# Second-half router transposes in a fourth PSUM bank, a surplus branch amid the last up products, and two SBUF buffers claimed later, in a two-layer transformer with 16 experts

## Chip, cores, metric

One core of one Trainium2 chip. The metric is the device time of one execution in microseconds, the median of several runs: 846.9 us before (three runs, 843.6 to 847.3).

## What is computed

x is 256 tokens of width 1024, in float32. Two layers, each a mixer and a mixture of experts, each followed by a layer norm:

```
h = x @ w_in                       # projections for three kinds of attention, and gates
m = sum_i sigmoid(gate_i) * (attention_i @ w_branch_i)
x = LN1(alpha*x + m @ w_o)
aff  = sigmoid(x @ router_w)       # 16 experts in 4 groups: the best group, then its 2 best experts
y    = sum_e combine[:, e] * ((silu(x @ w_gate[e]) * (x @ w_up[e])) @ w_down[e])
x = LN2(alpha*x + y)
```

Each expert has 6 MB of weights, and all 16 are read in each layer.

## The kernel before

**Buffers.** SBUF holds 25 equal buffers of 1 MB (`slot`, line 229). They serve everything large: raw weights as loaded (kind "w") and intermediate tensors (kind "o"). The program counts both kinds. `pump` (line 299) issues weight loads in a fixed order as long as fewer than 25 minus `target["o"]` weight buffers are held, and `put` (line 308) gives buffers back and pumps. The counts decide where in the program a load stands. Which buffer it gets is decided by order of release: the one that was let go earliest in the program. All weight loads stand in SP's queue, in order; each waits there until the last reader of its buffer has finished.

**End of a mixer** (lines 845 to 896). The last product is `m @ w_o`, in the stages 58 and 59 of 60 at the end. Their products for tokens 0 to 127 (t=0) go first; VectorE adds the result to x (`added`) and takes statistics, GpSimd makes the reciprocal deviation, and meanwhile TensorE does the products for t=1. The router's logits (`logits`, line 783) are computed from x before the norm: TensorE transposes x in blocks of 128 columns into a PSUM bank (step 0), ScalarE copies them to SBUF (`xT`), and TensorE multiplies by the router weights (step 1). For the last half of t=1 the transposes go in two halves, since each half of x is ready at its own time. Both halves use one bank, pT[1]. There are four "mm" banks (`pmm`), two "sc" (`psc`) and two "tp" (`ptp`). `normed` (line 429) writes the normed x to zk with one ScalarE activation and copies it to x1h, rounded to float32r. The difference zk - x1h is x1l (`low`).

**Start of the experts** (`moe`, lines 961 to 1063). VectorE forms the affinities from the logits (aff), finds the chosen experts (msk), and from them the one-hot matrix Sx[0]; a product with the constant prev (pc) counts positions. ScalarE does the exponential and then the three other `normed` quarters. `gather` (line 1037) multiplies x1h and x1l by Sx to fetch each expert's tokens, up to 32 per 128 tokens. Results go to two buffers xe, evacuated in turn by ScalarE (even k) and VectorE (odd k). `warm` are transposes that fill TensorE's wait.

**Experts** (lines 1314 to 1374). The 16 experts go in pairs p = 0 to 7: gate products (`up_("g", p)`), up products (`up_("u", p)`), and the down products of the pair before (`down(p - 1)`). Each takes four buffers of 1 MB, in two steps q of two. `scatter` adds results back to the tokens; scatter(2, 0) and scatter(2, 1) are those of the pairs 4 and 5, both made during pair 7. At p = 7 `target["o"]` is set to 16, so few loads of the next layer stand before the layer's end.

**Surplus branch** (`over`, lines 1195 to 1247). If an expert has more than 32 tokens in a half, a branch on all engines recomputes the surplus. It isn't taken with these inputs. Each engine loads the flag, compares and jumps, and waits for its own earlier instructions; SP waits for all loads that it has issued. The branch claims a buffer (wov) and eight PSUM banks. In layer 0 it stands after pair 7's up products and scatter(2, 1), in layer 1 ahead of pair 7's gate products.

Of the kernel before, what the change touches and what calls it, by code (L numbers as in the profile page):

```python
# [20 lines left out]
T = 2  # L21
# [183 lines left out]
def kernel(ctx: ExitStack, tc: tile.TileContext, x, w_in, a_w_uk, a_w_uv, c_sinks, w_branch,  # L205
# [78 lines left out]
    def load_one(pieces=1):  # L284
        key, src, shape = loads[nxt[0]]
        nxt[0] += 1
        t = loaded[key] = slot(shape, F32, "w_" + "_".join(map(str, key)), kind="w")
# [141 lines left out]
    def normed(zk, x1h, sc, shs, t, k):  # L429

        xv, zv = xt[0].rearrange("p t (q k) -> p t q k", k=KD), zk.rearrange("p t k q -> p t q k")
        A.activation(zv[:, t, :, k:k + 4], xv[:, t, :, k:k + 4], AF.Identity, bias=shs[t], scale=sc[t][1])
        A.copy(x1h[:, t, k:k + 4], zk[:, t, k:k + 4])


    def mixer(l, todo):
# [346 lines left out]
        def logits(t, j, step, ks=range(4)):  # L783

            if step == 0:
                if ks[0] == 0:
                    pT[t], xT[t] = ptp(), work()
# [13 lines left out]
        for i, (c, q) in enumerate(stages):  # L801
# [43 lines left out]
            if i >= len(stages) - 2:  # L845

# [34 lines left out]
                x1h = slot([128, T, KD, 128], F32R, "x1h")  # L881
                normed(zk, x1h, sc, shs, 0, 0)
                for h in range(2):
                    for kk in range(2):
                        part(*tail[1], 1, kk, h)
                    added(1, slice(256 * h, 256 * h + 256), pa[c][1 + h][:, :256])
                halves = (range(2), range(2, 4))
                logits(1, 1, 0, halves[0])
                logits(0, 1, 1)
                logits(1, 1, 0, halves[1])  # L890
                logits(1, 1, 1, halves[0])
                logits(1, 1, 1, halves[1])
                sc += ln_scales(st[1:])
                shs.append(ln_shift(*sc[1], E=G, name="sh1"))
                drop(3)
# [65 lines left out]
    def moe(l, sc, shs, lg, rsum, zk, xh):  # L961
        target["o"] = 5
# [10 lines left out]
        z = [aff[:, NE * t:NE * t + NE] for t in range(T)]  # L973
        low(0, 0)
        for t in range(T):
            V.scalar_tensor_tensor(z[t], rsum[:, 0:NE], sc[t][0], lg[t][:, 0:NE], op0=OP.mult, op1=OP.subtract)
        for t in range(T):
            V.scalar_tensor_tensor(z[t], z[t], sc[t][1], rsum[:, NE:2 * NE], op0=OP.mult, op1=OP.subtract)
        A.activation(aff, aff, AF.Exp)
        for t, k in ((1, 0), (0, 4), (1, 4)):  # L980
            normed(zk, xh, sc, shs, t, k)
# [55 lines left out]
        def gather(r, ks=range(KD)):  # L1037

            if r not in xe:
                z = [slot([128, 4, 8, T, CAP], F32, "xe") for i in range(2)]  # L1040
                xe[r] = [z[k // 4][:, k % 4] for k in range(KD)]
            for k in ks:
                o = (ptp if k % 2 == 0 else psc)()
# [14 lines left out]
        target["o"] = 4  # L1058
        pump()
# [121 lines left out]
        def up_(nm, p, o):  # L1181
# [4 lines left out]
            for q in range(2):  # L1186
# [5 lines left out]
                if (nm, p, q) == ("g", 0, 0):  # L1192
                    gather(0, range(4, KD))

        def over():

            flag = nc.values_load(fi[0:1, 0:1], min_val=0, max_val=1)
            clk.on = False
            with tc.If(flag > 0, label=f"over{l}"):  # L1199
                cov = small(32, "cov")  # L1200
                ec, ce, o1, o2 = small(1, "ec"), small(2, "ce"), small(16, "o1"), small(16, "o2")
                wt4 = slot([128, 4, 512], F32, "wov")
                ws, xs = ([wt4[:, z + i] for i in range(2)] for z in (0, 2))
                pg, pu = [pmm(), pmm()], [pmm(), pmm()]
                pt, po = [ptp(), ptp()], [psc(), psc()]
                V.scalar_tensor_tensor(cov, pos, NEG * (1024 + cap), comb, op0=OP.is_lt, op1=OP.mult)
                V.memset(ec, 0.0)
                with tc.For_i(0, NE, 1) as e:
# [28 lines left out]
                    for n in range(2):  # L1237
# [7 lines left out]
                        for t in range(T):  # L1245
                            s = xt[0][:, t, 512 * n:512 * n + 512]
                            V.scalar_tensor_tensor(s, po[t], ce[:, t:t + 1], s, op0=OP.mult, op1=OP.add)

# [65 lines left out]
        for p in range(NE // 2):  # L1314
# [9 lines left out]
            if p == 7:  # L1324
                target["o"] = 16
                if l == depth - 1:
                    over()
                    drop(3)
                    clk.on = True
# [11 lines left out]
            if p == 7:  # L1341
                scatter(2, 0)
# [10 lines left out]
            if p == 7:  # L1353
                if l < depth - 1:
                    over()
                    drop(3)
                    clk.on = True
# [55 lines left out]
```

## Time and profile before

| what | value |
|---|---|
| median of three runs | 846.9 us (847.3, 846.9, 843.6) |
| the profiled execution | 840.26 us, span 838.3 us |
| granted TensorE clock, mean | 0.997 |
| TensorE busy | 810.7 us (97% of the span) |
| VectorE, ScalarE, GpSimd busy | 429.7, 293.2, 87.5 us |
| read from HBM | 263.39 MB, 315 GB/s over the span |

Times in the profile count from the span's start. In the names of tiles, w_g, w_u and w_d are gate, up and down weights, w_in the projections' weights, pm, ps and pt the PSUM banks of the three kinds, xt and acc the residual x in layers 0 and 1, wt the working tiles (xT among them), and cst the constants (a product pt<-cst alone is a warm transpose). PE is TensorE, DVE is VectorE, ACT is ScalarE, SP is the engine that issues the loads. A busy TensorE is not one at its peak.

### The profile page before, as it was taken

Reading aid. Unit: us, or ns where it says so; the run is one execution under the profiler, and the core shown is the slowest. Engines: PE = TensorE matmul, PEld = TensorE weight load, DVE = VectorE, ACT = ScalarE, POOL = GpSimd, SP = SyncE. Lnnn points to the kernel's source line nnn. Section 1 sums busy time; section 2 is a strip of 40 time slices with the busy share of each in tenths; the row PEclk is TensorE's granted clock in tenths of the full one; section 3 lists DMA queues with packets and bytes.
Section 4 is the critical chain, followed back from the end, with each engine's and each line's share of the span. In section 5 each row is a group of like instructions: output and inputs, shape, how many; then the busy total and the mean of one; then the engine's idle time right before and its main releaser. Section 6 shows DMA issues by size and latency. Waiting matters only on the chain.

```text
span 838.3 us, 11334 instructions
## 1 busy us (share of the span) xinstructions
PE 810.7 (97%) x4365; PEld 500.9 (60%) x4365; DVE 429.7 (51%) x896; ACT 293.2 (35%) x509; POOL 87.5 (10%) x88
## 2 busy tenths in 40 slices
PE   7999999999999999998999999999999999999986
PEld 7888778888443433332588877888874334333333
DVE  5898565785331323223489976549662422222244
ACT  5545667344211211100454476653341112111112
POOL 1222221000030000000122132100000200000001
PEclk9999999999999999999999999999999999999998
DMA  9993336994899999999899414478939999999992
GB/s 313 345 386 132 132 121 208 394 353 150 305 420 420 419 420 418 419 421 419 324 387 327 156 56 146 155 273 340 367 131 376 419 420 420 419 419 420 417 412 80
DMA packets 65115, 265.24 MB, mean 316 GB/s; under 512 B 6880, under 2 KB 11168, under 8 KB 40992
## 3 DMA queue, kind: packets, MB, share of 16 engines
q1 hardware_dynamic: 64912, 264.39, 80.8%
q8 instruction: 36, 0.59, 0.3%
q14 instruction: 23, 0.19, 0.1%
q10 hardware_dynamic: 144, 0.07, 0.0%
HBM read 263.39 MB, written 1.05 MB: 315 GB/s over the span
## 4 chain that ended last, share of the span: by engine, by line
PE 42%; DMA 7%; DVE 2%; ACT 1%; POOL 0%; issue 0%; POOLq 0%; SPq 0%; ACTq 0%
PE pm L163 35%; DMA w_d<-in_moe_w_down_dram 5%; PE pt L163 4%; PE ps L163 3%; DMA w_u<-in_moe_w_up_dram 2%; DVE bm L163 1%; DVE acc L163 1%; DVE hl L163 0%; POOLq L1409 0%; POOL acc L163 0%; ACT zk L163 0%; POOL rstd L163 0%; ACT hl L163 0%; ACT acc L163 0%; DVE mv L163 0%
## 5 line engine op out<-in xcount | busy, mean ns | idle before, releaser
L163 PE MATMUL pm<-hl,xh 128*128 128x512 f32 (+2 forms) x704 | 226.6, 389 | 1.5 <-ACT hl L163 1.3
L163 PEld LDWEIGHTS pm<-hl,xh 128*128 128x128 f32 x704 | 131.5, 189 | 29.1 <-issue 4.2
L163 DVE TENSOR_TENSOR hl<-w_in,hl 128x1024 fp32r<-128x1024 f32 (+2 forms) x86 | 104.8, 1228 | 60.3 <-ACT hl L163 57.7
L163 PE MATMUL pm<-hl,xl 128*128 128x512 f32 (+2 forms) x352 | 133.9, 380 | 0.3 <-DVE xl L163 0.3
L163 PE MATMUL pm<-w_d,he 128*64 128x512 f32 x512 | 119.4, 597 | 4.2 <-DVEq L1199 2.8
L163 PE MATMUL pm<-w_g,xe 128*64 128x512 f32 x512 | 115.3, 594 | 3.2 <-DVEq L1199 1.7
L163 PE MATMUL pm<-w_u,xe 128*64 128x512 f32 x512 | 114.9, 593 | 1.7 <-DMA w_u<-in_moe_w_up_dram 1.7
L163 ACT CAST hl<-w_in 128x1024 fp32r<-128x1024 f32 (+2 forms) x88 | 85.8, 1001 | 6.5 <-DMA w_in<-in_w_in_dram 5.7
L163 PEld LDWEIGHTS pm<-w_g,xe 128*64 128x64 f32 x512 | 36.9, 137 | 76.5 <-issue 71.2
L163 PEld LDWEIGHTS pm<-w_u,xe 128*64 128x64 f32 x512 | 37.8, 137 | 74.4 <-issue 69.0
L163 PEld LDWEIGHTS pm<-w_d,he 128*64 128x64 f32 x512 | 36.9, 137 | 72.9 <-issue 66.6
L163 PEld LDWEIGHTS pm<-hl,xl 128*128 128x128 f32 x352 | 66.9, 190 | 10.1 <-DVE xl L163 0.5
L163 DVE SCALAR_TENSOR_TENSOR he<-he,pm 128x512 f32<-128x512 f32 x16 | 17.0, 1063 | 87.6 <-ACT he L163 78.9
L163 DVE TENSOR_TENSOR he<-he,pm 128x512 f32<-128x512 f32 x16 | 17.1, 1069 | 67.4 <-PE pm L163 67.4
L163 ACT COPY he<-pm 128x512 f32<-128x512 f32 x14 | 8.2, 586 | 109.9 <-PE pm L163 109.9
L163 ACT ACTIVATE he<-pm 128x512 f32<-128x512 f32 x16 | 17.3, 1078 | 80.6 <-PE pm L163 80.6
L163 PE MATMUL pm<-hl,mh 128*128 128x512 f32 (+1 forms) x160 | 45.0, 355 | 0.0
L163 DVE SCALAR_TENSOR_TENSOR yt<-pm,cs,yt 128x512 fp32r<-128x512 f32 x32 | 22.9, 747 | 43.0 <-ACT yt L163 42.1
L163 ACT ACTIVATE yt<-pm,cs 128x512 fp32r<-128x512 f32 x32 | 20.8, 685 | 67.4 <-PE pm L163 67.4
L163 PE MATMUL pm<-hl,oh 128*128 128x512 f32 x128 | 41.3, 394 | 0.0
L163 POOL TENSOR_TENSOR un<-un,su 128x512 f32<-128x512 f32 x24 | 30.7, 1283 | 95.2 <-DVE su L163 57.0
L163 POOL TENSOR_TENSOR wt<-wt 128x256 f32<-128x256 f32 (+1 forms) x36 | 27.3, 772 | 107.5 <-DVE wt L163 99.9
(193 smaller groups left out, 989.9 us busy)
## 6 DMA issues: line engine op xcount, KB each, us to landing
w_g<-in_moe_w_gate_dram SPq DMA_DIRECT2D x64, 1024.0 KB, 13.7
w_u<-in_moe_w_up_dram SPq DMA_DIRECT2D x64, 1024.0 KB, 14.5
w_d<-in_moe_w_down_dram SPq DMA_DIRECT2D x60, 1024.0 KB, 19.1
w_in<-in_w_in_dram SPq DMA_DIRECT2D x36, 1024.0 KB, 13.5
w_br<-in_w_branch_dram SPq DMA_DIRECT2D x8, 1024.0 KB, 5.1
w_wo<-in_w_o_dram SPq DMA_DIRECT2D x8, 1024.0 KB, 5.1
w_d<-in_moe_w_down_dram SPq DMA_DIRECT2D x8, 512.0 KB, 17.1
w_in<-in_w_in_dram SPq DMA_DIRECT2D x4, 768.0 KB, 8.1
```

Of the source, the lines that this page charges most:

```text
L163: r = f(*args, **kw)
```

## The change

- In `logits`, the second half of t=1's transposes goes to a bank of its own, taken from the "mm" kind, and the products follow once for all four blocks.
- `normed` makes zk alone, with the two orders of its access pattern exchanged: it now writes zk contiguously and reads x with a stride of 8 elements, where before it read runs of 4 elements and wrote with a stride of 128. `high` makes x1h. For the first quarter, `high` stands behind the copies of the logits' transposes.
- x1h is claimed after the three buffers of the mixer's end are given back, and the first half and second half of xe are claimed one by one. `target["o"]` becomes 5 at the stages 58 and 59, and 4 at the start of `moe`, where it was 6 until the end of the mixer, 5 at the start of `moe` and 4 behind the first gather.
- In `moe` the four affinity operations of VectorE stand t by t ahead of low(0, 0), not behind it.
- scatter(2, 0) stands between the two steps of pair 7's gate products, and the branch between the two steps of its up products, in both layers. The branch's scratch counts as a weight buffer; the next layer's next load goes into it. Its accumulators share one bank more.

```diff
-    def load_one(pieces=1):
+    def load_one(pieces=1, t=None):
         key, src, shape = loads[nxt[0]]
         nxt[0] += 1
-        t = loaded[key] = slot(shape, F32, "w_" + "_".join(map(str, key)), kind="w")
+        if t is None:
+            t = slot(shape, F32, "w_" + "_".join(map(str, key)), kind="w")
+        else:
+            t = t.rearrange("p a b -> p (a b)")[:, :shape[1] * shape[2]].rearrange("p (a b) -> p a b", a=shape[1])
+        loaded[key] = t
...
-    def normed(zk, x1h, sc, shs, t, k):
-
-        xv, zv = xt[0].rearrange("p t (q k) -> p t q k", k=KD), zk.rearrange("p t k q -> p t q k")
-        A.activation(zv[:, t, :, k:k + 4], xv[:, t, :, k:k + 4], AF.Identity, bias=shs[t], scale=sc[t][1])
+    def normed(zk, sc, shs, t, k):
+
+        A.activation(zk[:, t, k:k + 4], xt[0][:, t].rearrange("p (q k) -> p k q", k=KD)[:, k:k + 4], AF.Identity,
+                     bias=shs[t], scale=sc[t][1])
+
+    def high(zk, x1h, t, k):
+
         A.copy(x1h[:, t, k:k + 4], zk[:, t, k:k + 4])
...
-        def logits(t, j, step, ks=range(4)):
+        def logits(t, j, step, ks=range(4), make=None):
 
             if step == 0:
                 if ks[0] == 0:
-                    pT[t], xT[t] = ptp(), work()
+                    xT[t] = work()
+                if ks[0] == 0 or make:
+                    pT[t] = (make or ptp)()
...
             if i >= len(stages) - 2:
+                target["o"] = 5
+                pump()
...
-                x1h = slot([128, T, KD, 128], F32R, "x1h")
-                normed(zk, x1h, sc, shs, 0, 0)
+                normed(zk, sc, shs, 0, 0)
                 for h in range(2):
                     for kk in range(2):
                         part(*tail[1], 1, kk, h)
                     added(1, slice(256 * h, 256 * h + 256), pa[c][1 + h][:, :256])
+                drop(3)
+                x1h = slot([128, T, KD, 128], F32R, "x1h")
                 halves = (range(2), range(2, 4))
                 logits(1, 1, 0, halves[0])
                 logits(0, 1, 1)
-                logits(1, 1, 0, halves[1])
-                logits(1, 1, 1, halves[0])
-                logits(1, 1, 1, halves[1])
+                logits(1, 1, 0, halves[1], pmm)
+                high(zk, x1h, 0, 0)
+                logits(1, 1, 1)
                 sc += ln_scales(st[1:])
                 shs.append(ln_shift(*sc[1], E=G, name="sh1"))
-                drop(3)
...
     def moe(l, sc, shs, lg, rsum, zk, xh):
-        target["o"] = 5
+        target["o"] = 4
...
-        low(0, 0)
-        for t in range(T):
-            V.scalar_tensor_tensor(z[t], rsum[:, 0:NE], sc[t][0], lg[t][:, 0:NE], op0=OP.mult, op1=OP.subtract)
-        for t in range(T):
-            V.scalar_tensor_tensor(z[t], z[t], sc[t][1], rsum[:, NE:2 * NE], op0=OP.mult, op1=OP.subtract)
-        A.activation(aff, aff, AF.Exp)
+        centred(0)
+        scaled(0)
+        centred(1)
+        scaled(1)
+        A.activation(aff, aff, AF.Exp)
+        low(0, 0)
...
-            if r not in xe:
-                z = [slot([128, 4, 8, T, CAP], F32, "xe") for i in range(2)]
-                xe[r] = [z[k // 4][:, k % 4] for k in range(KD)]
             for k in ks:
+                if k % 4 == 0:
+                    z = slot([128, 4, 8, T, CAP], F32, "xe")
+                    xe.setdefault(r, []).extend(z[:, i] for i in range(4))
...
-        target["o"] = 4
-        pump()
...
                 if (nm, p, q) == ("g", 0, 0):
                     gather(0, range(4, KD))
+                if (nm, p, q) == ("g", 7, 0):
+                    scatter(2, 0)
+                if (nm, p, q) == ("u", 7, 0):
+                    wt4 = over()
+                    drop(2)
+                    if l + 1 < depth:
+                        load_one(1, wt4)
+                    else:
+                        drop(1, "w")
+                    clk.on = True
 
         def over():
+            wt4 = slot([128, 4, 512], F32, "wov", kind="w")
...
-                wt4 = slot([128, 4, 512], F32, "wov")
-                pg, pu = [pmm(), pmm()], [pmm(), pmm()]
                 pt, po = [ptp(), ptp()], [psc(), psc()]
+                pg, pu = [pmm(), pmm()], [pmm(), po[1]]
...
             if p == 7:
                 target["o"] = 16
-                if l == depth - 1:
-                    over()
-                    drop(3)
-                    clk.on = True
...
-            if p == 7:
-                scatter(2, 0)
             up_("u", p, pu)
...
-            if p == 7:
-                if l < depth - 1:
-                    over()
-                    drop(3)
-                    clk.on = True
```

## Rows read from the trace of the kernel before

**Rows 1.** Busy time by stage: each stretch in us, its length, then busy time (and instructions) of PE, PEld (weight loads), DVE, ACT and POOL, the granted clock, the DMA engines' share and GB/s. The stretches are the mixer's end and the experts' start, the experts with TensorE never idle, and the experts' end, for layer 0 and then (without the second) layer 1.
```profile
194.00:222.00 28.00, 26.93 (x189) 20.50 (x190) 14.31 (x48) 12.44 (x17) 1.70 (x4) 1.00 0.51 180
222.00:360.00 138.00, 138.00 (x716) 53.13 (x714) 39.32 (x61) 20.74 (x29) 7.52 (x2) 1.00 1.01 417
360.00:410.00 50.00, 44.84 (x226) 16.20 (x224) 15.60 (x21) 6.69 (x9) 0.00 (x0) 1.00 0.98 397
606.00:634.00 28.00, 26.94 (x188) 20.80 (x189) 14.32 (x48) 12.34 (x18) 1.68 (x4) 1.00 0.52 183
...
780.00:818.00 38.00, 34.20 (x171) 13.31 (x164) 14.76 (x20) 6.31 (x8) 0.00 (x0) 1.00 1.01 413
```

**Rows 2.** Who waited for whom, for TensorE over the whole span: us in total, times, longest. DVEq L1199 is VectorE's sequencer at the surplus branch.
```profile
PE pm L163 <- DVEq L1199: 4.5, 2, 2.8
...
PE pt L163 <- ACT wt L163: 1.9, 2, 1.0
```

**Rows 3.** TensorE in order of time, at the experts' start of layer 0: start and duration in us, and in brackets the idle time before and what ended it. The last line is the same place in layer 1.
```profile
201.26 0.96 PE L163 MATMUL ps<-rwg,wt 128*128 128x16 f32 x8
203.18 0.44 PE L163 MATMUL pt<-cst,xt 128*128 128x128 f32 x2 [0.96 <-ACT wt L163]
...
210.17 0.28 PE L163 MATMUL pt<-Sx,x1l 128*128 128x256 f32 x1
...
211.85 0.65 PE L163 MATMUL pm<-w_g,xe 128*64 128x512 f32 x2
...
615.85 0.44 PE L163 MATMUL pt<-cst,acc 128*128 128x128 f32 x2 [0.95 <-ACT wt L163]
```

**Rows 4.** ScalarE in order of time, same place in layer 0.
```profile
199.80 0.59 ACT L163 COPY wt<-pt 128x512 f32<-128x512 f32 x1 [5.88 <-PE pt L163]
200.93 1.28 ACT L163 ACTIVATE zk<-xt,sh,rstd 128x512 f32<-128x512 f32 x1 [0.54 <-DVE xt L163]
202.24 0.62 ACT L163 CAST x1h<-zk 128x512 fp32r<-128x512 f32 x1
202.76 0.36 ACT L163 COPY wt<-pt 128x256 f32<-128x256 f32 x1
203.66 0.37 ACT L163 COPY wt<-pt 128x256 f32<-128x256 f32 x1 [0.53 <-PE pt L163]
205.34 0.23 ACT L163 ACTIVATE aff<-aff 128x32 f32<-128x32 f32 x1 [1.31 <-DVE aff L163]
...
211.02 1.44 ACT L163 ACTIVATE xe<-pt,gpk 128x512 f32<-128x512 f32 x2
```

**Rows 5.** VectorE in order of time, same place in layer 0.
```profile
201.31 0.41 DVE L163 SCALAR_TENSOR_TENSOR xt<-xt,pm 128x256 f32<-128x256 f32 x1
...
202.89 0.69 DVE L163 TENSOR_TENSOR x1l<-zk,x1h 128x512 fp32r<-128x512 f32 x1 [0.23 <-ACT x1h L163]
...
204.74 0.23 DVE L163 SCALAR_TENSOR_TENSOR aff<-rsum,mv,ps 128x16 f32<-128x16 f32 x1 [1.01 <-PE ps L163]
204.89 0.42 DVE L163 SCALAR_TENSOR_TENSOR aff<-aff,rstd,rsum 128x16 f32<-128x16 f32 x2
205.61 0.18 DVE L163 TENSOR_SCALAR aff<-aff 128x32 f32<-128x32 f32 x1 [0.30 <-ACT aff L163]
```

**Rows 6.** SP in order of time: single loads (the last one of w_d for pair 0, and two of w_g for pair 2, layer 0), and the first load of layer 1's w_in behind the branch.
```profile
201.10 0.33 SPq L221 DMA_DIRECT2D w_d<-in_moe_w_down_dram  x1
...
210.49 0.33 SPq L221 DMA_DIRECT2D w_g<-in_moe_w_gate_dram  x1
...
221.22 0.33 SPq L221 DMA_DIRECT2D w_g<-in_moe_w_gate_dram  x1
...
409.96 0.38 SPq L221 DMA_DIRECT2D w_in<-in_w_in_dram  x1
```

**Rows 7.** TensorE's weight products in order of time, pair 7 and the down products of pairs 6 and 7, layer 0.
```profile
377.22 3.65 PE L163 MATMUL pm<-w_g,xe 128*64 128x512 f32 x14 [1.33 <-DMA w_g<-in_moe_w_gate_dram]
...
387.36 3.65 PE L163 MATMUL pm<-w_u,xe 128*64 128x512 f32 x14 [0.92 <-DMA w_u<-in_moe_w_up_dram]
394.91 0.65 PE L163 MATMUL pm<-w_d,he 128*64 128x512 f32 x2 [2.75 <-DVEq L1199]
...
408.15 1.08 PE L163 MATMUL pm<-w_d,he 128*64 128x512 f32 x4
```

**Rows 8.** The same for layer 1.
```profile
785.72 7.95 PE L163 MATMUL pm<-w_g,xe 128*64 128x512 f32 x32 [1.70 <-DVEq L1199]
...
800.00 3.65 PE L163 MATMUL pm<-w_u,xe 128*64 128x512 f32 x14 [0.76 <-DMA w_u<-in_moe_w_up_dram]
...
814.99 1.51 PE L163 MATMUL pm<-w_d,he 128*64 128x512 f32 x6 [1.34 <-DMA w_d<-in_moe_w_down_dram]
```

**Rows 9.** Groups of instructions over the whole span, shapes apart: busy us in total, mean ns of one, idle time before and what ended it. The first writes he with a stride, the second writes it contiguously; the third reads two scale operands and writes contiguously, and the last reads x1h and x1l with a stride, on GpSimd.
```profile
L163 ACT ACTIVATE he<-pm 128x512 f32<-128x512 f32 x16 | 17.3, 1078 | 80.6 <-PE pm L163 80.6
...
L163 ACT COPY he<-pm 128x512 f32<-128x512 f32 x14 | 8.2, 586 | 109.9 <-PE pm L163 109.9
...
L163 ACT ACTIVATE xe<-pt,gpk 128x512 f32<-128x512 f32 x16 | 12.2, 776 | 21.7 <-PE pt L163 21.7
...
L163 POOL TENSOR_TENSOR acc<-x1h,x1l 128x1024 f32<-128x1024 f32 x4 | 15.1, 3783 | 62.6 <-PE pm L163 62.6
```

More of the change, by code (lines that the diff above doesn't have):

```diff
@@ L973, in moe, with centred, scaled @@
         z = [aff[:, NE * t:NE * t + NE] for t in range(T)]
-        low(0, 0)
-        for t in range(T):
-            V.scalar_tensor_tensor(z[t], rsum[:, 0:NE], sc[t][0], lg[t][:, 0:NE], op0=OP.mult, op1=OP.subtract)
-        for t in range(T):
-            V.scalar_tensor_tensor(z[t], z[t], sc[t][1], rsum[:, NE:2 * NE], op0=OP.mult, op1=OP.subtract)
-        A.activation(aff, aff, AF.Exp)
+        def centred(t):
+            V.scalar_tensor_tensor(z[t], rsum[:, 0:NE], sc[t][0], lg[t][:, 0:NE], op0=OP.mult, op1=OP.subtract)
+        def scaled(t):
+            V.scalar_tensor_tensor(z[t], z[t], sc[t][1], rsum[:, NE:2 * NE], op0=OP.mult, op1=OP.subtract)
+        centred(0)
[3 more added lines that the diff above has]
+        A.activation(aff, aff, AF.Exp)
+        low(0, 0)
         for t, k in ((1, 0), (0, 4), (1, 4)):
-            normed(zk, xh, sc, shs, t, k)
+            normed(zk, sc, shs, t, k)
+            high(zk, xh, t, k)
         drop()
@@ L1247, in over @@
                             V.scalar_tensor_tensor(s, po[t], ce[:, t:t + 1], s, op0=OP.mult, op1=OP.add)
+            return wt4
         o, parts, stm = {}, [], []
```

## The prediction, made before the changed kernel was run

> **What bounds the kernel now.** I read the busy time by stage first. TensorE is busy for 97% of the span, so only stages where it idles can give anything. Those are the passages from mixer to experts (1.1 us idle of 28 in each layer) and the experts' ends (5.2 us of 50 in layer 0, 3.8 of 38 in layer 1) [rows 1]. In the experts' stretches the reader should look at the last two columns: the DMA engines are full and move 413 to 417 GB/s, so a 1 MB buffer (1.049 MB) lands every 2.5 us. In the passages they are half empty (180 GB/s).
>
> Next, TensorE's waits: 4.5 us for VectorE at the surplus branch, and 1.9 us for ScalarE's copies of the logits' transposes [rows 2].
>
> Then the engines in order of time. At the passage TensorE waits 0.96 us for the copy that frees the shared bank [rows 3]. From there one chain sets the experts' start: ScalarE's copy (203.66), the logits, VectorE's affinities (204.74), the exponential (205.34), then ScalarE without a pause through three normed quarters to the first xe (211.02), and the first gate product at 211.85 [rows 3 to 5].
>
> At the experts' ends TensorE has caught up with the loads: it resumes at 377.22, 387.36, 800.00 and 814.99 on a landing [rows 7, 8].
>
> So the experts are bound like this: the load at 221.22 waits for a buffer that TensorE's gate products of pair 0 let go [rows 6]. From the landing of this load on the DMA engines are full until the layer's end. The end is therefore the experts' start plus a fixed time, and **a microsecond off the start is a microsecond off the end**, while one saved at the end mostly runs into the next landing.
>
> **The change part by part.**
>
> *Logits' bank.* Before, ScalarE's order is zk (ends 202.21), x1h, the copy of the first half, a wait for TensorE, the copy of the second [rows 4]. Now the second half's transposes need only x, ready at 201.72 [rows 5], and TensorE, free at 203.18 - 0.96 = 202.22 [rows 3]; they end at 202.66. The first copy moves up to 202.24, the second goes at 202.70 instead of 203.66: 0.96 us gained. x1h (0.62 us) follows at 203.07, in ScalarE's wait for the affinities (1.31 us before [rows 4]).
>
> *Affinities.* They come at 203.78 instead of 204.74. One of the two scaled operations (the pair takes 0.42 us [rows 5]) now precedes the logits' arrival, so 0.15 to 0.2 us more leaves the chain. The exponential goes at about 204.2, 1.1 us earlier.
>
> *low(0, 0) behind them.* This adds a wait: it takes 0.69 us of VectorE [rows 5] ahead of the next affinity operation, which then starts at about 204.9 instead of 205.61, 0.7 earlier. Behind it stand the choice of experts, Sx and the gather: its first block, done at 210.45 [rows 3], would be done at 209.75. ScalarE reaches xe at 211.02 - 1.1 = 209.92, still last. So VectorE's smaller gain is covered, by 0.2 us. With 0.8 us of xe behind it, the gate products start at 210.75 instead of 211.85.
>
> *zk's access pattern.* ScalarE's contiguous write takes 586 ns, the same size with a strided write 1078, so the stride costs 0.49 us [rows 9]. zk takes 1.28 [rows 4]; the contiguous activation with two scale operands, 776 ns [rows 9], plus 0.49 is 1.27, so reading runs of four costs nothing. The trace has no ScalarE operation with a strided read. The nearest rows: 776 ns if it is free; on GpSimd two strided reads take 3783 ns for 1024 columns, 1.89 us for 512 [rows 9], the upper end. I take 1.28, unchanged, a single stride's price as for the write. At 776 ns the normed chain shrinks by 1.5 us, but VectorE's gather (209.75) then bounds: 0.2 us more per layer. At 1.89 us zk stands four times in the chain: 4 x 0.61 = 2.4 us, less the 0.1 of slack that the first copy leaves: 2.3 us per layer lost.
>
> The Trainium skill (SBUF — State Buffer, section "Door 1: The DMA port swizzle", the note on 16-byte cachelines) says that each access to a new line pays and four fp32 values share one. By that, the read with a stride of 32 bytes pays as the write did, and the sum stays as below; taken as free, it would be 0.4 us lower over both layers.
>
> *Buffers and loads.* The last w_d of pair 0 is issued earlier than 201.10, behind stage 57, and the first w_g of pair 2 at about 201.3 instead of 210.49 [rows 6], as their buffers are let go by the mixer's last products. The load after these waits for zk's last reader, and the one at 221.22 for pair 0's gate products, as before: the number of weight buffers from the first gather on is the same. So two loads move within an idle stretch of the DMA engines, and the saturated stream starts with the same load. Worth nothing by itself. New waits: zk takes stage 58's buffer, last read ahead of the transposes copied at 199.80 [rows 4]; x1h that of the mixer's low part, read until TensorE's logits; xe's first half that of x, read until ScalarE's last zk. All end before they are asked for. GpSimd's queue isn't passed.
>
> *scatter(2, 0)* goes into a stretch where TensorE idles 1.33 us for w_g [rows 7]; the next step resumes on a landing anyway. Nothing in either layer.
>
> *The branch.* It frees TensorE of 2.75 us at 394.91 and 1.70 at 785.72 [rows 7, 8]. In its new place VectorE reaches it right after pair 7's gate activation, ahead of TensorE's first use of a bank behind it. TensorE's own part, between 0 and 1.70 us (the whole idle time in layer 1 [rows 8]), I put at 0.5, low in that span since VectorE is named as the one that ended both waits; 0.92 and 0.76 us of waiting for w_u cover it [rows 7, 8]; uncovered it costs what exceeds them. What is late next: in layer 0 the loads. The last w_u lands at 387.3, the next four at 2.5 us each: 397.3 for w_d of pair 6, 402.3 for the second buffer of pair 7. The down products then go at 402.3 + 3.6 + 1.9 (the rest's products) = 407.8 instead of 408.15 [rows 7]: 0.3 us of 2.75. In layer 1 the wait for w_d at 814.99 takes all 1.70. SP's branch stands behind the same load as before, so it waits for the same landings, and the first load behind it, now into the scratch, keeps its place at 409.96 [rows 6].
>
> *Sum.* 1.1 us at each experts' start (the row at 615.85 shows the same wait in layer 1 [rows 3]) and 0.3 at layer 0's end: 2.5 us. The profiled execution's 840.3 us would be 837.8. It is 6.6 us below the median of the runs, so I take the difference: 846.9 - 2.5 = **844.4 us**. A measurement of this kernel tells 0.5%, 4.2 us, from no change; this is less.
>
> **The rivals.**
>
> *The early loads pay.* If moving them up by 8 to 9 us really advanced the stream by one buffer, each layer's end would come 2.5 us earlier, covered by the idle 5.2 and 3.8 us there [rows 1]: 2 x 2.5 more, 839.4. For it: half-empty DMA engines in the passage. Against it: the load at 221.22 waits for TensorE, not for the queue.
>
> *The strided read is dearer.* The place is zk, four times per layer in the chain. At 1.89 us: 2 x 2.3 - 2.5 = 2.1 us slower, 849.0. It decides from about 1.6 us on, where 2 x 4 x 0.3 = 2.4 us eat the gain. For it: GpSimd's row. Against it: one read here, two there, and another engine.
>
> *The branch in mid-product stalls TensorE.* The Trainium skill (Runtime: NRT & Kernel Launch, "Instruction fetch mechanics") says that a taken branch whose target isn't in the two pages held waits for a fetch. No row shows a stall of its own: what there is lies within the 1.70 us. As a mechanism here: 1.70 instead of 0.5 exceeds the cover by 0.8 and 0.9 us, which layer 0 gives back out of the freed 2.75 and layer 1 out of the 1.34 us ahead of 814.99 [rows 8]. Time: 844.4 to 844.7. It shows in the trace rather than in the time.
>
> *The change does less than it says:* if the second transposes still waited for the first copy, in spite of their own bank, only x1h's 0.52 us ahead of the copies and the 0.15 of the affinities would go per layer: 2 x 0.67 + 0.3 = 1.6, 845.3.
>
> **How the numbers follow.** My forecast has 0.62, the stall 0.06, the early loads 0.12, the dearer read 0.12, the lesser change 0.08. Runs of one kernel spread over 3.7 us, so a case's measured time lies within some 2 us of it. Low: 840.8 leaves out the lower part of the early loads' case. High: 848.5 leaves out the upper half of the dearer read's. Faster by over 0.5%: the early loads nearly whole (0.11) and 0.11 of the forecast by the spread, 0.22. Slower by over 0.5% (above 851.1): the dearer read at its upper end with the spread, 0.04. Within: 0.74.
>
> **What would show it.** Right: TensorE's 0.96 us wait before the second transposes gone; two ScalarE copies back to back ahead of x1h; the first gate product 1.1 us earlier against the mixer's last product in both layers; no DVEq wait at the branch, but longer waits for w_d instead. Wrong: zk not near 1.28 us; the stretch from the first gate product to the layer's end not the same to 0.4 us; a wait of over 1 us in mid up product of pair 7.

## The result and the profile after

| | median us | runs | lowest to highest |
|---|---|---|---|
| before | 846.86 | 6 | 840.6 to 847.3 |
| after | 839.44 | 6 | 838.56 to 840.89 |

The ratio of the runs is 0.9935, with an interval of 0.9905 to 0.9964: faster by 0.65%. By these two medians it is 7.4 us. The forecast was 844.4 us (840.8 to 848.5). The ratio puts the kernel after at 841.4 us against the 846.9 that the forecast started from, inside the range; the median of its own runs lies 1.4 us below it. The likeliest case, a change within 0.5%, is neither met nor ruled out: the interval reaches from 0.36 to 0.95% faster. One run of the kernel before, at 1178.99 us with a mean clock of 0.654, is left out of every figure below.

The two profiled executions say something else: their spans are 838.4 us (after) and 838.3 us (before). The question is why the profiles agree and the medians differ.

First the busy time by stage of the kernel after, in the columns and stretches of [rows 1].

```profile
194.00:222.00 28.00, 27.93 (x194) 21.15 (x194) 14.25 (x48) 13.13 (x18) 1.66 (x4) 1.00 0.50 185
222.00:360.00 138.00, 138.00 (x716) 53.14 (x712) 39.32 (x61) 20.72 (x29) 7.53 (x2) 1.00 1.01 417
360.00:410.00 50.00, 47.40 (x226) 18.06 (x224) 15.79 (x21) 6.94 (x10) 0.00 (x0) 1.00 0.98 397
606.00:634.00 28.00, 27.95 (x197) 21.72 (x197) 14.25 (x48) 12.95 (x18) 1.64 (x4) 1.00 0.53 186
780.00:818.00 38.00, 35.44 (x171) 13.35 (x168) 14.84 (x20) 6.27 (x8) 0.00 (x0) 1.00 1.01 413
```

TensorE's idle time at the passages is gone (1.07 to 0.07 us in layer 0), and at the experts' ends it falls from 5.2 to 2.6 us and from 3.8 to 2.6. Next, the passage in order of time: TensorE (the last two lines are layer 1), then ScalarE, then VectorE. These answer to [rows 3 to 5].

```profile
202.09 0.96 PE L163 MATMUL ps<-rwg,wt 128*128 128x16 f32 x8
202.90 0.42 PE L163 MATMUL pm<-cst,xt 128*128 128x128 f32 x2
...
210.13 0.28 PE L163 MATMUL pt<-Sx,x1l 128*128 128x256 f32 x1
...
211.80 1.08 PE L163 MATMUL pm<-w_g,xe 128*64 128x512 f32 x4
...
615.77 0.42 PE L163 MATMUL pm<-cst,acc 128*128 128x128 f32 x2
...
624.63 1.94 PE L163 MATMUL pm<-w_g,xe 128*64 128x512 f32 x8
```

```profile
201.76 1.32 ACT L163 ACTIVATE zk<-xt,sh,rstd 128x512 f32<-128x512 f32 x1 [0.55 <-DVE xt L163]
202.98 0.35 ACT L163 COPY wt<-pt 128x256 f32<-128x256 f32 x1
203.36 0.37 ACT L163 COPY wt<-pm 128x256 f32<-128x256 f32 x1
203.62 0.62 ACT L163 CAST x1h<-zk 128x512 fp32r<-128x512 f32 x1
205.09 0.23 ACT L163 ACTIVATE aff<-aff 128x32 f32<-128x32 f32 x1 [0.85 <-DVE aff L163]
...
210.91 1.44 ACT L163 ACTIVATE xe<-pt,gpk 128x512 f32<-128x512 f32 x2
```

```profile
204.83 0.23 DVE L163 SCALAR_TENSOR_TENSOR aff<-aff,rstd,rsum 128x16 f32<-128x16 f32 x1
204.98 0.68 DVE L163 TENSOR_TENSOR x1l<-zk,x1h 128x512 fp32r<-128x512 f32 x1
205.58 0.17 DVE L163 TENSOR_SCALAR aff<-aff 128x32 f32<-128x32 f32 x1
```

Times must be taken from a common point, because this execution arrives at the passage 0.83 us late (zk at 201.76, not 200.93 [rows 4]). From zk to the exponential are 3.33 us instead of 4.41, to xe 9.15 instead of 10.09, to the first gate product 10.04 instead of 10.92. So the exponential gains 1.08 us and the gate products 0.88. TensorE's second transposes no longer wait, and the two copies stand back to back ahead of x1h.

TensorE at the experts' ends (layer 0, then layer 1), against [rows 7, 8]:

```profile
386.14 4.70 PE L163 MATMUL pm<-w_u,xe 128*64 128x512 f32 x16 [0.28 <-PEq L1228]
...
402.21 3.65 PE L163 MATMUL pm<-w_d,he 128*64 128x512 f32 x14 [1.36 <-DMA w_d<-in_moe_w_down_dram]
...
407.83 3.65 PE L163 MATMUL pm<-w_d,he 128*64 128x512 f32 x16
...
795.05 8.62 PE L163 MATMUL pm<-w_u,xe 128*64 128x512 f32 x30 [0.77 <-DMA w_u<-in_moe_w_up_dram]
...
815.01 3.65 PE L163 MATMUL pm<-w_d,he 128*64 128x512 f32 x14 [1.33 <-DMA w_d<-in_moe_w_down_dram]
```

No wait names VectorE's sequencer any more. At the branch TensorE is idle for 0.28 us in layer 0. That isn't all of its price: the row at 795.05, with the branch in it, takes 8.62 us for 30 products, where [rows 8] has 32 in 7.95. A wait of 1.36 us for w_d has come in layer 0, and that of layer 1 is unchanged. From the first gate product to the last down step, layer 0 takes 196.03 us instead of 196.30.

Then the granted clock behind layer 1's start (windows of 4 us, columns as above), and TensorE there:

```profile
418.00:422.00 4.00, 2.49 (x20) 1.95 (x18) 3.96 (x6) 1.89 (x4) 2.88 (x2) 1.00 1.05 388
422.00:426.00 4.00, 3.69 (x15) 3.25 (x15) 2.17 (x4) 0.85 (x2) 0.00 (x0) 0.57 1.04 386
```

```profile
420.97 0.63 PE L163 MATMUL pt<-cst,acc 128*128 128x128 f32 x4 [1.51 <-DVE acc L163]
...
423.43 0.74 PE L163 MATMUL pm<-hl,xh 128*128 128x324 f32 x2
```

The granted clock is 0.57 on average over these 4 us: most of them at the lower level, 1.2 GHz. Pairs of products that take 0.46 us at the full clock take 0.74. TensorE had just been idle for 1.51 us. The profiled execution of before had the same idle stretch and kept its clock:

```profile
421.29 0.63 PE L163 MATMUL pt<-cst,acc 128*128 128x128 f32 x4 [1.51 <-DVE acc L163]
```

```profile
422.00:426.00 4.00, 3.46 (x24) 2.96 (x23) 2.62 (x5) 1.92 (x4) 0.28 (x1) 1.00 1.04 387
```

So the profiles balance like this (after minus before): 0.83 us lost in the first 15 us, where the programs are identical; 0.88 gained at layer 0's passage; 0.27 at its end; 1.35 lost from there to layer 1's passage; 0.91 gained at that passage (10.81 us before, 9.90 after, from the first of the logits' last transposes to the gate product); 0.10 at layer 1's end. The sum is 0.02 us lost, with over 2 us won by the change.

The 0.83 us at the start are the clock's too. TensorE's first transposes and products of each execution go at the lower level: a pair of products takes 0.74 us there, as in the fall above, and 0.46 a little later. The level rises at another moment in each execution. TensorE around that moment, before and then after:

```profile
9.98 0.74 PE L163 MATMUL pm<-hl,xh 128*128 128x324 f32 x2
...
11.06 1.07 PE L163 MATMUL pt<-cst,xt 128*128 128x128 f32 x8
...
12.27 0.45 PE L163 MATMUL pm<-hl,xh 128*128 128x324 f32 x2
```

```profile
11.11 1.80 PE L163 MATMUL pt<-cst,xt 128*128 128x128 f32 x8
```

The same eight transposes take 1.07 us in one execution and 1.80 in the other. The column of the clock shows 1.00 throughout, because the trace's record of the clock begins only with the rise, at 11.12 us before and 12.65 after. In all twelve profiles the record begins between 10.53 and 13.67 us, and the first zk starts between 200.64 and 202.22: about half a microsecond later for each microsecond that the rise comes later.

### The profile page after: what moved, and what is told of

The parts are those of the page before. It is cut to its first block, busy times and chain, and to the rows that moved or that the text cites. A ratio compares the mean times of both kernels' runs of the same rounds, so it can differ in the third digit from the quotient of the medians.

```text
span 838.4 us, 11339 instructions
## 1 busy us (share of the span) xinstructions
PE 816.8 (97%) x4365; PEld 504.7 (60%) x4365; DVE 430.0 (51%) x896; ACT 293.5 (35%) x509; POOL 87.6 (10%) x88
## 4 chain that ended last, share of the span: by engine, by line
PE 81%; DMA 15%; DVE 2%; ACT 1%; POOL 0%; issue 0%; POOLq 0%; SPq 0%; ACTq 0%
PE pm L163 68%; DMA w_d<-in_moe_w_down_dram 9%; PE pt L163 8%; PE ps L163 5%; DMA w_u<-in_moe_w_up_dram 5%; DVE bm L163 1%; DVE hl L163 1%; DVE acc L163 1%; DMA cst<-in_consts_dram 0%; ACT hl L163 0%; ACT zk L163 0%; POOLq L1427 0%; POOL acc L163 0%; POOL rstd L163 0%; DVE ml L163 0%
## 5 line engine op out<-in xcount | busy, mean ns | idle before, releaser
L163 DVE TENSOR_TENSOR hl<-w_in,hl 128x1024 fp32r<-128x1024 f32 (+2 forms) x84 | 103.1, 1238 | 60.4 <-ACT hl L163 57.7
L163 PE MATMUL pm<-w_u,xe 128*64 128x512 f32 x512 | 117.3, 593 | 2.1 <-DMA w_u<-in_moe_w_up_dram 1.5
## 6 DMA issues: line engine op xcount, KB each, us to landing
w_g<-in_moe_w_gate_dram SPq DMA_DIRECT2D x64, 1024.0 KB, 13.7
```

The costliest lines, as they stand in the source:

```text
L163: r = f(*args, **kw)
```

## The experiments

**First: which part, and do the runs differ by the clock?** Four kernels: before once more, and each of the three parts alone on top of before. *Passage* has the change's `normed`, `high` and `logits`, and `low(0, 0)` behind the affinities; in its core:

```diff
-                logits(1, 1, 0, halves[1])
-                logits(1, 1, 1, halves[0])
-                logits(1, 1, 1, halves[1])
+                logits(1, 1, 0, halves[1], pmm)
+                high(zk, x1h, 0, 0)
+                logits(1, 1, 1)
```

*Branch* has the change's `up_` and `over`:

```diff
+                if (nm, p, q) == ("g", 7, 0):
+                    scatter(2, 0)
+                if (nm, p, q) == ("u", 7, 0):
+                    wt4 = over()
```

*Loads* has the change's targets, and its claims of x1h and xe:

```diff
+                target["o"] = 5
+                pump()
...
-        target["o"] = 5
+        target["o"] = 4
```

> The kernel before once more, unchanged, for the granted clock and the time of each of its runs (the runs listed so far give 840.6 to 847.3 us and no clock). Three theories on why the change gains 7 us by the medians and only 2.5 us by my sum. Theory of the clock: in some executions the granted clock falls to its lower level for about 3.4 us behind an idle stretch of TensorE (the trace of after has one such fall, at 422 us, behind 1.51 us of idle, and the trace of before has none). One fall of 3.4 us at half speed takes 1.7 us off the work and 0.002 off the mean clock (1.7 of 838); then runs near 847 us should show a mean clock 0.006 to 0.008 lower than runs near 840 us, and the times should lie on steps of about 1.3 to 1.7 us. Theory of the stream: in the runs of 847 us weights land later, TensorE waits for them at the same clock: the mean clock differs by less than 0.002 between runs of 840 and of 847 us. Theory of the chain alone: the scatter is chance and the medians differ by 2 to 3 us once more runs are taken, here a median near 843 us.

> The kernel before with one part of the change alone: the logits in two PSUM banks, the copy of the states behind the logits' copies, low(0, 0) behind the affinities and the exchanged access patterns of zk; loads and branch stay where they were. Chain alone: 0.9 us less per layer, so 1.8 us below the kernel before, 845.1 at a median of 846.9. Clock: the 0.96 and 0.95 us waits ahead of the second transposes go, but the branch's 2.75 and 1.70 us stay, so it may lose some falls of the clock at the two passages: 1.8 us and up to two falls of 1.3 to 1.7, 842 to 845. Stream: 0 to 1.8 us, as without the loads' earlier start nothing lands earlier.

> The kernel before with the surplus branch and scatter(2, 0) moved amid the up products and the scratch in the next weights' buffer, nothing else. Chain alone: 0.3 us in layer 0 and 0 to 0.1 in layer 1, so 846.5 at a median of 846.9. Clock: TensorE's idle of 2.75 and 1.70 us goes, and with it the falls behind them: if most of the extra 5 us hangs on these two places, 842 to 844; a fall behind each costs 1.3 to 1.7 us, so two falls give no more than 3.4. Stream: 846.9, unchanged to 0.3.

> The kernel before with the claims and loads alone: targets 5 and 4, the pump at the two stages, x1h claimed behind the drop, the halves of xe claimed one by one; logits, copies and branch as before. Chain alone and clock: no gain, 846.9 to within 0.5 (two loads start 7 to 8 us earlier and land long before they are read). Stream: the two weights per layer that start 7 to 8 us earlier let the whole stream run ahead: 840 to 842.

| kernel | median us | lowest to highest | ratio to before (interval) | mean clock of the runs |
|---|---|---|---|---|
| before again | 843.64 | 840.24 to 847.54 | 0.9998 (0.9972 to 1.0024) | 0.988 to 0.997 |
| passage | 841.06 | 840.46 to 841.65 | 0.9957 (0.9935 to 0.9979) | 0.992 to 0.996 |
| branch | 842.29 | 840.28 to 845.01 | 0.9976 (0.9954 to 0.9998) | 0.992 to 0.998 |
| loads | 842.83 | 840.22 to 847.64 | 0.9981 (0.9954 to 1.0009) | 0.988 to 0.997 |

The runs of the kernel before lie on three steps, and the mean clock names the step. Over all 104 runs of it taken with these experiments, 23 lie at 840.05 to 841.55 us (mean clock 0.997 to 0.998), 48 at 842.66 to 844.89 (0.993 to 0.995), and 33 at 846.14 to 847.87 (0.988 to 0.991). The theory of the stream needed the same clock on all steps, so it falls. This time the profile fell on the middle step. Windows of the kernel before, run again (843.28 us), with the two idle stretches ahead of the falls:

```profile
204.00:208.00 4.00, 4.00 (x25) 4.00 (x25) 3.01 (x20) 2.91 (x4) 0.00 (x0) 0.64 0.22 90
208.00:212.00 4.00, 4.00 (x34) 3.84 (x33) 1.68 (x6) 2.86 (x5) 0.00 (x0) 0.94 0.26 47
...
396.00:400.00 4.00, 3.90 (x11) 1.47 (x13) 0.00 (x0) 0.00 (x0) 0.00 (x0) 0.57 1.03 416
```

```profile
202.90 0.44 PE L163 MATMUL pt<-cst,xt 128*128 128x128 f32 x2 [0.97 <-ACT wt L163]
...
213.20 1.08 PE L163 MATMUL pm<-w_g,xe 128*64 128x512 f32 x4
...
396.10 1.89 PE L163 MATMUL pm<-w_d,he 128*64 128x512 f32 x4 [2.76 <-DVEq L1199]
```

From the second transposes to the first gate product it takes 10.30 us instead of 8.67 [rows 3]: one fall costs 1.6 us there. The first profile of before has the same idle stretch [rows 3] and no fall behind it. Two falls make 843.3 out of 840.4. The top step would be four by its mean clock; none of the profiled executions lies on it.

The loads alone keep all three steps (five, four and three runs), and their lowest runs are those of before: **the early loads are worth nothing.** The branch alone keeps two steps of six runs each, 840.41 and 844.14 us in the middle; its profile has a fall behind the 0.97 us of layer 0's passage and one of double length behind layer 1's 0.96 us:

```profile
618.00:622.00 4.00, 3.89 (x19) 3.80 (x19) 2.26 (x13) 2.24 (x5) 0.00 (x0) 0.52 0.37 152
622.00:626.00 4.00, 4.00 (x25) 4.00 (x24) 1.59 (x10) 3.54 (x4) 0.00 (x0) 0.63 0.07 14
```

The passage alone has no run above 841.65, yet none below 840.46 either, and none at 0.997. Here the mean clock does not name the time: five runs at 0.992 to 0.994 and seven at 0.996 lie at 841.2 and 841.0 us in the middle. Its profile (841.65) has falls at the two places that it leaves: the branch, and layer 1's start (windows of 4 us):

```profile
392.00:396.00 4.00, 2.01 (x6) 0.86 (x8) 1.73 (x3) 0.00 (x0) 0.00 (x0) 0.69 1.02 416
...
422.00:426.00 4.00, 3.46 (x18) 2.92 (x17) 2.97 (x5) 1.22 (x2) 0.75 (x1) 0.78 1.05 388
```

**Second: the clock by itself, the bank, and a better version.** In *cover* nothing of the change is done; the idle stretches of before are only filled:

```diff
             turn_x(0, t)
+            if l > 0 and t == 0:
+                warm(12, pmm)
...
                 logits(0, 1, 1)
+                warm(8, pmm)
                 logits(1, 1, 0, halves[1])
...
                 if l == depth - 1:
+                    warm(12, pmm)
                     over()
...
                 if l < depth - 1:
+                    warm(20, pmm)
                     over()
```

*No bank* is after without the second bank:

```diff
-                logits(1, 1, 0, halves[1], pmm)
+                logits(1, 1, 0, halves[1])
```

*Better* is after with these edits:

```diff
             turn_x(0, t)
+            if l > 0 and t == 0:
+                warm(12, pmm)
...
-        low(0, 0)
+        low(0, 0, 2)
...
-            high(zk, xh, t, k)
+            if (t, k) != (1, 4):
+                high(zk, xh, t, k)
...
-        low(1, 0)
+        low(1, 0, 2)
...
+        low(0, 2, 2)
+        low(1, 2, 2)
...
         gather(0, range(4))
+        high(zk, xh, 1, 4)
```

> The kernel after once more, unchanged, to have its runs beside those of the kernel before on one chip. Shown so far: the runs of before lie on three steps, 840.4, 843.4 and 847.0 us, at mean clocks of 0.997, 0.993 to 0.994 and 0.988 to 0.990; falls of 3.4 us to the lower level stand in the traces behind the idle of 0.97 us at layer 0's passage, of 2.76 us at the branch and of 1.51 us at layer 1's start, and each puts the later work 1.5 to 1.65 us back. Theory of the clock: after has only one place left for a fall, the 1.51 us at layer 1's start, so two steps, 838.6 (0.997) and 840.4 (0.996), nothing above 841.5, median 838.6 to 840.4. If the scatter has another cause: some of 12 runs above 842.

> The kernel before, with TensorE's idle stretches filled by transposes of the identity that nobody reads, and nothing else changed: 8 ahead of the second transposes at each passage (0.96 and 0.95 us idle), 20 ahead of the branch in layer 0 (2.75), 12 ahead of it in layer 1 (1.70), 12 at layer 1's start (1.51), 0.11 us each. Theory of the clock: the chains stay as long as before, the falls go; all runs near the fastest of before, 840.3 to 841.3, median about 840.6, mean clock 0.996 to 0.998, none above 842. If the gain is the chains' and the loads' own: no gain, or 0 to 1 us worse, median 843 to 847 with the three steps still there.

> The kernel after with the second transposes of the logits back in the shared bank (the copy of the states stays behind the logits' copies). Chain: TensorE waits again for the first copy, but for 0.35 to 0.4 us, not 0.96, as the 0.62 us copy of the states no longer stands between; the exponential 0.3 later than in after, +0.3 per layer, 0.5 us in all against after. Clock: if 0.4 us of idle is enough for a fall, some runs 1.5 to 3 us above those of after; if it isn't, the same two steps as after, 0.5 higher.

> The kernel after with three edits: 12 needless transposes in the 1.51 us of TensorE's idle at layer 1's start; low(0, 0) and low(1, 0) halved, the first halves where VectorE waits (0.36 us each in place of 0.68), the second halves behind the first one-hots; the copy of the fourth block of the states behind the first gather's activations. Chain: the aff chain no longer waits 0.22 us for low(0, 0), nor the one-hots 0.05 for low(1, 0): 0.25 us per layer, 0.5 in all. Clock: no place for a fall is left, so one step only, 838.0 to 838.6, mean clock 0.997, median 838.1. If falls do not hang on the idle: the two steps of after stay, 838.1 and 839.9.

| kernel | median us | lowest to highest | ratio to before (interval) | mean clock of the runs |
|---|---|---|---|---|
| after again | 838.96 | 838.31 to 841.2 | 0.9957 (0.9937 to 0.9977) | 0.994 to 0.998 |
| cover | 841.35 | 840.28 to 842.76 | 0.9984 (0.9966 to 1.0002) | 0.997 to 0.998 |
| no bank | 841.19 | 839.14 to 841.87 | 0.9963 (0.9942 to 0.9984) | 0.995 to 0.998 |
| better | 838.62 | 837.51 to 839.8 | 0.995 (0.9932 to 0.9968) | 0.996 to 0.998 |

*Cover* is the test that decides. All 12 runs have a mean clock of 0.997 or 0.998, that of the lowest step of before, while 81 of the 104 runs of before have a lower one on the upper steps. By time 11 of the 12 lie below the middle step, and one (842.76) at its lower edge. All this although every chain is as long as before and the branch still stands. Its windows, at the places where the others fell:

```profile
204.00:208.00 4.00, 3.89 (x34) 3.79 (x35) 2.52 (x13) 2.20 (x4) 0.41 (x2) 1.00 0.49 201
...
396.00:400.00 4.00, 4.00 (x22) 1.65 (x20) 0.00 (x0) 0.10 (x1) 0.00 (x0) 1.00 1.01 410
...
618.00:622.00 4.00, 4.00 (x39) 4.00 (x39) 3.25 (x22) 3.18 (x4) 0.00 (x0) 1.00 0.15 64
```

Its median is 0.75 us above the expected 840.6, it scatters over 2.5 us, and three runs lie above 842, where none was expected. In its profile 0.8 us of delay against the first profile of before are there by 182 us and stay to the end, ahead of every edit in the order of work: the clock's record begins at 13.04 us, 1.92 later than in before.

*After again* has two steps as expected, 838.3 to 839.1 and 840.4 to 841.2, and nothing above. *No bank* shows what the bank is worth: TensorE waits 0.32 us, the gate product comes 10.48 us behind zk instead of 10.04, 0.44 per layer, where 0.3 was expected. The lower step rises by 1.0 us (839.71 in the middle of five runs, 838.68 in the ten of after), and there is an upper step of seven runs; the idle stretch at layer 1's start is still there too, so the runs don't say where each of the seven fell. The one profile shows a fall behind even 0.32 us of idle, in layer 1's passage, where after waits for nothing (the same wait in layer 0, 0.33 us, has no fall behind it):

```profile
615.34 0.44 PE L163 MATMUL pt<-cst,acc 128*128 128x128 f32 x2 [0.32 <-ACT wt L163]
```

```profile
616.00:620.00 4.00, 3.89 (x22) 3.79 (x22) 2.79 (x14) 3.17 (x6) 0.35 (x2) 0.60 0.54 215
```

*Better* has no run above 839.8; its median is 0.5 us above the expected 838.1. Its edits of the chain did what was expected: VectorE's next affinity operation starts 0.26 us behind the exponential (204.44) instead of 0.49, and the gate product comes 0.23 us earlier against the exponential. In its profile (a span of 837.4 us) the experts of layer 1 take 1.2 us more than in after again, with a wait of 1.27 us for w_d at 774.07 that after again doesn't have.

```profile
204.32 0.42 DVE L163 TENSOR_TENSOR x1l<-zk,x1h 128x256 fp32r<-128x256 f32 x1
204.70 0.18 DVE L163 TENSOR_SCALAR aff<-aff 128x32 f32<-128x32 f32 x1
```

**Third: the rest of after's scatter, and zk's access pattern.** Two kernels on top of after: the 12 transposes at layer 1's start alone, and the old access patterns alone.

```diff
             turn_x(0, t)
+            if l > 0 and t == 0:
+                warm(12, pmm)
```

```diff
-        A.activation(zk[:, t, k:k + 4], xt[0][:, t].rearrange("p (q k) -> p k q", k=KD)[:, k:k + 4], AF.Identity,
-                     bias=shs[t], scale=sc[t][1])
+        xv, zv = xt[0].rearrange("p t (q k) -> p t q k", k=KD), zk.rearrange("p t k q -> p t q k")
+        A.activation(zv[:, t, :, k:k + 4], xv[:, t, :, k:k + 4], AF.Identity, bias=shs[t], scale=sc[t][1])
```

> The kernel after with one edit: 12 transposes of the identity that nobody reads in TensorE's 1.51 us of idle at layer 1's start. In the 18 runs of after so far 10 lie at 838.3 to 839.1 us and 8 at 840.1 to 841.2, and the one profile among the upper ones has its fall of the clock behind this idle. Theory of the clock: the upper step goes, all runs at 838.3 to 839.5, median 838.7. If the upper step has another cause (a late landing, say): about half the runs stay at 840.1 to 841.2.

> The kernel after with the access patterns of zk exchanged back: strided write and runs-of-four read in place of contiguous write and strided read. My forecast held the two equal (1.28 us); the trace of after has the new form at 1.317 to 1.340 us, 0.05 dearer. Three of them stand in ScalarE's chain, so the first activation of the gathered states comes 0.1 to 0.15 us earlier per layer; but TensorE's own gather ends at the same time, so 0 to 0.1 us per layer on the end: the time of after within 0.3. Rival (the pattern matters to VectorE, which reads zk for low): low slower than its 0.68 us, and the gain lost.

| kernel | median us | lowest to highest | ratio to before (interval) | mean clock of the runs |
|---|---|---|---|---|
| warm | 838.70 | 837.72 to 840.25 | 0.9928 (0.9905 to 0.9951) | 0.996 to 0.998 |
| old zk | 839.68 | 838.46 to 840.83 | 0.9952 (0.9933 to 0.9972) | 0.994 to 0.997 |

*Warm*: ten of 12 runs lie at 837.7 to 839.1, and no run is at 0.994 or 0.995 any more, so after's upper step was the idle stretch at layer 1's start. With *better*, which has the same transposes there, one of 24 runs lies above 840 us; of after's 18 it was eight. Two runs of *warm* (839.67 and 840.25) lie higher at 0.997 and 0.998. The first is the profiled one, and it has no fall: the clock rises latest of all the profiles (13.67 us), zk starts at 202.22, 0.84 us later than in the profile of after again, and the span is 0.85 us longer.

```profile
11.11 1.91 PE L163 MATMUL pt<-cst,xt 128*128 128x128 f32 x8
```

*Old zk* still has four runs at 0.994 and goes up to 840.83, as after does. ScalarE's zk, all instructions of a layer (ns, lowest, median and highest), first with the old patterns, then in after:

```profile
L163 ACT ACTIVATE zk<-xt,sh,rstd x4: 1292/1298/1312, 201.1 to 208.3; 128x512 f32<-128x512 f32 x4
```

```profile
L163 ACT ACTIVATE zk<-xt,sh,rstd x4: 1317/1335/1340, 201.8 to 209.0; 128x512 f32<-128x512 f32 x4
```

The old form is 37 ns cheaper, and its lowest runs (838.46 to 838.78) are those of after: worth nothing on the end.

## Where the prediction was right and where it failed

*The chain: right as far as the exponential, 0.2 us too large behind it.* Forecast 1.1 us per layer at the gate products, measured 0.88 and 0.91. The exponential gained the 1.1 (1.08). What failed is "So VectorE's smaller gain is covered, by 0.2 us". It was not covered. With low(0, 0) ahead, VectorE's next operation starts 0.49 us behind the exponential, where it was 0.27 [rows 4, 5]. So the gather's second block gained 0.87 us against zk (8.37 instead of 9.24), and the gate products gained as much: they start 1.68 us behind that block before (210.17 [rows 3]) and 1.67 after (210.13). *Better*, which halves low(0, 0), moved both by another 0.2.

The term "1.28, unchanged" for zk was off as well: it is 1.33 us, and three of them put xe 0.14 us later behind the exponential. But this didn't reach the gate products. In *old zk*, where zk starts at 201.13, xe comes 8.99 us behind it instead of 9.15, and the first gate product 9.96 instead of 10.04:

```profile
210.12 1.44 ACT L163 ACTIVATE xe<-pt,gpk 128x512 f32<-128x512 f32 x2
```

```profile
211.09 0.65 PE L163 MATMUL pm<-w_g,xe 128*64 128x512 f32 x2
```

Of the two ends given for the strided read, free and 1.89 us, neither came. The Trainium skill (SBUF — State Buffer, section "Door 1: The DMA port swizzle", the note on 16-byte cachelines) was cited for a strided read that pays as the strided write did; this case's traces agree to 0.05 us (1335 ns against 1288).

*Layer 0's end: between 0 and the forecast.* Forecast 0.3 us of the 2.75; 0.27 in the first profile of after, 0.02 in the second (196.28 us from the gate product to the last down step), and 0.19, 0 and 0 in *no bank*, *warm* and *old zk*. The freed time went into waits for w_d, 1.36 and 1.40 us, as the prediction said. Layer 1 gave 0.1 where 0 was forecast.

*The branch: right.* TensorE's own part was put at 0.5 us. It is 0.28 of idle in layer 0, beside 0.78 of waiting for w_u, and at least 0.67 us with the slower products around it in layer 1 (8.62 us for 30 of them instead of 7.95 for 32). That is less than the 1.70 of the rival that the branch stalls TensorE in mid-product; no idle stretch of 1 us stands there.

*The loads: right, and the rival met the time by chance.* The load of [rows 6] at 221.22 goes at 221.19 in after:

```profile
202.05 0.33 SPq L221 DMA_DIRECT2D w_g<-in_moe_w_gate_dram  x1
...
221.19 0.33 SPq L221 DMA_DIRECT2D w_g<-in_moe_w_gate_dram  x1
```

The early loads' case gave 839.4 us, and 839.4 was measured, but the loads alone move nothing. A time that fits does not prove its mechanism.

*The sum against runs with no fall: 1.9 us instead of 2.5.* The middle of the lowest step of before is 840.56 us (23 runs), that of after 838.68 (10 of 18). The profiles say nearly the same without the first 200 us, 1.7 to 1.9: from the first zk to the end of the span it is 637.4 us in the two without a fall that have the old chains (before, *cover*), and 635.6 to 635.7 in three that have the new ones (*after again*, *warm*, *old zk*).

*The step that failed for the time* is the last one: "It is 6.6 us below the median of the runs, so I take the difference". That carried the 6.6 us over to the new kernel as if they were its own. They were falls of the granted clock, which the profiled execution did not have, behind the very waits that the change removes. I had costed these waits by the chain alone, and the branch's at nearly nothing, since the next landing hides them; that they also bring a lower clock in some executions stood in no row of that profile. Only the spread of 840.6 to 847.3 us hinted at it, and I used it as noise.

In numbers: the mean of the 104 runs of before is 843.97 us, 3.4 above its lowest step; that of the 18 runs of after is 839.55, 0.9 above its own. Of the 4.4 us between the means, 1.9 are the shorter chain by the lowest steps, and 2.5, the rest, are put down to the falls that no longer happen. The 7.4 us of the first medians are more than this because four of those six runs of before lay on the top step, where a third of all lie.

Shown: that the steps of before are the clock's (their mean clocks, and the windows of the profiles with and without falls); that filling the idle stretches takes the falls away with all else left as it was (*cover* for before, *warm* for after); that the loads are worth nothing; that without falls the time still moves with the moment of the clock's first rise. Not shown: why the clock falls behind the same idle stretch in one execution and not in the next; that the top step holds four falls; that the mean clock counts falls one by one (the middle step holds runs at 0.993 and at 0.995, 843.4 and 843.0 us in the middle); why the passage alone never reached the lowest step; and whether the first rise makes all of the remaining 2 us of scatter, since only the profiled executions show it.

## What to carry to other kernels

One profile shows one execution: where the runs spread by more than the repeats of one would, compare the mean clock of each run with its time before giving the distance between the profile and the median to the next kernel. A short wait of TensorE has two prices, its place in the chain and the chance that the clock falls behind it. Where the chain can't be shortened, transposes that nobody reads, in the wait, buy the second price back: 12 of them took after's upper step away. When two profiles are compared, take the times from a point behind the start: the start alone moved the first zk by 1.6 us here.

## What the runs showed of the hardware

- The granted clock fell from 2.4 to 1.2 GHz for about 3.4 us (0.64 and 0.94 in two windows of 4 us, 0.57 in another), once for twice that, behind idle stretches of TensorE of 0.97, 2.76, 1.51 and, in one profile, 0.32 us; one such fall cost 1.2 to 1.7 us. The kernel before had none in one profiled execution and two in another.
- Each execution began at 1.2 GHz, by its products' durations (0.74 us for a pair, 0.46 later), and rose to 2.4 GHz between 10.5 and 13.7 us, with TensorE at work on transposes and first products since 4.05 us. The eight transposes at 11.1 us took 1.07, 1.80 and 1.91 us in three of them.
- The Trainium skill (TensorE: Matmul & The Clock Gate, section "What's actually happening") says that the clock follows how busy TensorE has lately been. The traces agree in kind: each fall begins within 2.5 us of the end of an idle stretch, or inside it.
- ScalarE paid 1298 ns for 512 columns with a strided write and 1335 with a strided read instead; without a stride the same size takes 776 [rows 9].
